# A fixed order on VectorE in the closing norm of each stage, held weight splits, and three smaller moves in a two-block transformer kernel

## The chip, the cores and the metric

The kernel runs on 1 core of one Trainium2 chip. The metric is the device time of one execution in microseconds (us); of several runs the median is taken. A core has five engines that work side by side, each on its own queue of instructions: TensorE (PE in the profile, its weight loads PEld), VectorE (DVE), ScalarE (ACT), GpSimd (POOL) and SyncE (SP). SP only issues transfers here.

## The reference, cut to what matters

The input is one sequence of 256 tokens with 1024 features, in fp32. Ten stages follow one another, and each ends in the same way:

```python
for l in range(2):
    x = layer_norm(ALPHA * x + 0.5 * swiglu(x, ffn1_w1[l], ffn1_w2[l]))   # 1024 -> 2 x 2816 -> 1024
    x = layer_norm(ALPHA * x + token_mix(x))      # three attention branches, each with its gate
    x = layer_norm(ALPHA * x + 0.5 * swiglu(x, ffn2_w1[l], ffn2_w2[l]))
for l in range(2):
    x = layer_norm(ALPHA * x + (ssd_mixer, dilated_attention)[l](x))
    x = layer_norm(ALPHA * x + moe(x))            # 32 experts, 2 per token, hidden 512
```

The third attention branch of token_mix subtracts from its scores a running sum over the tokens of `log_sigmoid(f + b_f)`; this sum is called its decay below.

## The kernel before, in words

**Products.** Every fp32 product is made of three products of parts. A raw weight tile of 1 MB comes by a transfer from SP into one of 4 buffers (`NRAW`). `split` (L63) makes of a piece of 128 x 2 x 512 a high part with a copy on ScalarE (L65) and a low part with a subtraction on VectorE (L66), in one of 7 split buffers (`NSPLIT`). `mm3` (L115) multiplies high by high (L116), high by low (L117) and low by high (L118). The activations lie transposed, as high part `xh` and low part `xl`.

**Feed-forward pass** (`ffn`, L275, four times). 11 groups of 256 columns. Group G does: gate_up(G) (L294), four splits and 48 products into one tile of two PSUM banks (`gu`); gating (L306), a tanh on ScalarE (L190) and two products on VectorE (L309, L310); then, from G = 2, the down products of group G - 2, 24 of them into four banks (`acc`, one for each half of 128 tokens and half of 512 columns); then `turned` (L313), which transposes the gated group (`hT`, L317) and splits it (L320, L321). So in groups 0 and 1 no down products lie between a gate/up sum and its transposes, and the one `gu` tile has to be read before the next sum begins. Behind the last group the down products of the last two groups are left as the tail.

**The end of a stage** (`finish`, L213). `tail_half` (L90) issues the last products, for token half t = 0, then 1; inside each k both column halves take turns, so that both end together. The tail is 4 k deep in feed-forward, 2 in token_mix (`MTAIL`, L846), 3 in SSD (`TAIL`, L1049), 2 in the dilated attention (`DTAIL`). For each token half VectorE then does, by column half, the residual sum (L241) and its statistics (L242), then the aggregation (L244); ScalarE a logarithm and an exponential (L247, L248); VectorE the centring of the whole row (L251), three small steps (L252 to L254) and, by column half, the scaling (L263; L260 where the columns are dealt out in another order). TensorE transposes each scaled half row (`turn_x`, `xps`, L181); ScalarE copies the high part (L183) and VectorE subtracts the low part (L184). The last norm of the program writes its rows out instead.

**Order.** The instructions of each engine are put in a fixed order when the program is built, by a list scheduler with its own cost estimates, which takes what it holds to be ready first. An edge of the kind `order` (L57) only fixes the order of two instructions in that list. The splits of the next stage, which need its weights alone, can be placed before, between or behind the instructions of a norm.

**Set-up in the first feed-forward pass.** At groups 2, 5 and 8 (`SETUPG`) parts of `setup_all` run: POOL loads constants, tables, parameters (`load_params`, `pars`) and the routers' weights `rw` (L1237, L1238). `router_parts` (L1243) splits `rw` into `rs` on ScalarE (L1246) and VectorE (L1247). It is called before the SSD and the dilated stage (L1603); the scheduler has placed the first call's two instructions into the first feed-forward pass.

**token_mix** (L435). The projections come in 256-column groups. The decay block (L670 to L677) stands before the compressed scores of the first branch: log_sigmoid in 17 small VectorE instructions and an exponential, two products with a triangle of ones (L673, L674), a negation (L675) and a store from ScalarE's queue. Its readers come in the third branch.

**MoE** (L1250). Behind the router's arithmetic, in which the tokens' places are gathered, 16 pairs of experts run at a steady pace. A pair does gate products `gps` and up products `ups` (L1430), tanh, two VectorE products (`t`, L1438, L1439), transposes (L1441), a copy on VectorE (`hT`, L1444), down products `yp` (L1453) and their copy (L1459), and adds to `eacc` (L1464) at the end of the stage. Its weights lie in 21 slots in a written order (`ORDER`, L23): 8 tiles in space freed by other things (a0 to a7), the 4 raw tiles (r), the 7 split buffers (s) and the two activation tiles (x0, x1). The last pair of the first MoE stage is followed by the splits of the dilated stage.

Of the kernel before, what the change touches and what calls it, by code (L numbers as in the profile page):

```python
# [10 lines left out]
F32 = mybir.dt.float32  # L11
# [30 lines left out]
def tile_stack(ctx: ExitStack, tc: tile.TileContext, a: dict, out: bass.AP):  # L42
# [89 lines left out]
    pars = const.tile([128, 256], F32)  # L132

    def load_params(pp, pq):
# [20 lines left out]
        for i in range(2):  # L155
            ps = pq.tile([128, 128], F32, tag="tr", name="ptr")
            nc.tensor.transpose(ps, stage[i], ident)
            nc.vector.tensor_copy(out=pars[:, i * 128:(i + 1) * 128], in_=ps)
# [18 lines left out]
    def turn_x(trp, t, hf, src, tag):  # L177
# [5 lines left out]
        nc.scalar.activation(out=X["h"][:, t, cs, :], in_=ps, func=AF.Copy)  # L183
        nc.vector.tensor_tensor(out=X["l"][:, t, cs, :], in0=ps, in1=X["h"][:, t, cs, :].bitcast(F32), op=ALU.subtract)  # L184
# [28 lines left out]
    def finish(accs, last, scale, g, b, trp, tag="tr", room=None, dealt=False, was_dealt=False, write=None, loaded=False):  # L213


        with pool(name="lnt", bufs=2) as tmp, ExitStack() as own:
# [15 lines left out]
            for t in range(2):  # L232
                st = tmp.tile([128, 2, 6], F32, tag="st", name="lnst")
                for hf in range(2):
                    hs = slice(hf * 512, (hf + 1) * 512)
                    k = X["k"][:, t, hs]
                    if was_dealt:
                        nc.vector.scalar_tensor_tensor(out=r[:, t, hs].rearrange("p (f k) -> p f k", k=4), in0=by_rows(k), scalar=ALPHA * scale,  # L238
                                                       in1=accs[t][hf].rearrange("p (f k) -> p f k", k=4), op0=ALU.mult, op1=ALU.add)
                    else:  # L240
                        nc.vector.scalar_tensor_tensor(out=r[:, t, hs], in0=k, scalar=ALPHA * scale, in1=accs[t][hf], op0=ALU.mult, op1=ALU.add)  # L241
                    nc.vector.bn_stats(out=st[:, hf, :], in_=r[:, t, hs])  # L242
                mv = tmp.tile([128, 2], F32, tag="mv", name="lnmv")
                nc.vector.bn_aggr(out=mv, in_=st)  # L244
                rs = tmp.tile([128, 1], F32, tag="rs", name="lnrs")
                nw = tmp.tile([128, 1], F32, tag="nw", name="lnnw")
                nc.scalar.activation(out=rs, in_=mv[:, 1:2], func=AF.Ln, bias=eps_t[scale], scale=1.0)  # L247
                nc.scalar.activation(out=rs, in_=rs, func=AF.Exp, scale=-0.5)  # L248
                if t == 1:
                    table("exp_and_others")  # L250
                nc.vector.scalar_tensor_tensor(out=r[:, t, :], in0=r[:, t, :], scalar=mv[:, 0:1], in1=gb[:, 0, :], op0=ALU.subtract, op1=ALU.mult)  # L251
                nc.vector.scalar_tensor_tensor(out=nw, in0=mv[:, 1:2], scalar=eps_t[scale], in1=rs, op0=ALU.add, op1=ALU.mult)  # L252
# [1414 lines left out]
```

## Time and profile before

| | before |
|---|---|
| time, median of 3 runs (lowest to highest) | 2876.24 us (2873.5 to 2877.69) |
| the profiled execution's own time | 2875.49 us |
| its span in the trace | 2873.7 us |
| mean granted TensorE clock | 0.97 |
| instructions in the span | 36446 |
| bytes moved by transfers | 710.37 MB, 247 GB/s over the span |

The span is the time from the first to the last instruction in the trace. A busy share is an engine's busy time over the span. The granted clock is TensorE's clock as a share of full speed (2.4 GHz); 0.50 is its lower level, 1.2 GHz. "A <- B" behind an idle time names what ended it.

### The profile page before, as it was taken

To read this page: it belongs to the slowest core of one execution; us is meant where nothing else is said; L and a number is where in the kernel's file an instruction comes from. 1 tells how busy PE (TensorE), PEld (TensorE's weight loads), DVE (VectorE), ACT (ScalarE), POOL (GpSimd) and SP (SyncE) were. 2 spreads that over 40 slices of the span, in tenths; PEclk is the share of its full clock that TensorE was granted. 3 is DMA by queue.
4 is the path that set the end of the run, shared out by engine and by line. 5 is a ranking of instruction groups with operands and counts; after the bars stand their busy time and mean duration, and the time that the engine had idled before them with its cause. 6 is when DMAs were issued, how large, how long until landed. Compare 5 with 4: busy or idle time off the path is not lost. (4 is left out here: it accounts for less than half of the span.)

```text
span 2873.7 us, 36446 instructions
## 1 busy us (share of the span) xinstructions
PE 2721.6 (95%) x14368; PEld 1890.8 (66%) x14368; DVE 1345.2 (47%) x2669; ACT 991.6 (35%) x1699; POOL 57.9 (2%) x124
## 2 busy tenths in 40 slices
PE   8799999899999999989989989999998989999997
PEld 6687688788788768878878854444436975444443
DVE  4466665655655566665578841111116662111112
ACT  3343555444444355544447710100014440000011
POOL 2100000000000000000000000000000000000000
PEclk9899999999999999999999989999998998999999
DMA  8765454565555645446555599999974468999993
GB/s 217 209 212 155 116 174 162 168 191 188 163 191 175 168 124 171 155 150 198 172 164 177 190 375 421 421 421 421 421 296 152 129 231 359 420 420 421 421 421 148
DMA packets 302944, 710.37 MB, mean 247 GB/s; under 512 B 21189, under 2 KB 212353, under 8 KB 253617
## 3 DMA queue, kind: packets, MB, share of 16 engines
q1 hardware_dynamic: 289920, 688.11, 65.7%
q10 hardware_dynamic: 10736, 14.80, 1.6%
q0 software_dynamic: 2112, 5.08, 1.2%
q8 instruction: 115, 1.88, 0.3%
q14 instruction: 61, 0.49, 0.1%
HBM read 706.81 MB, written 4.27 MB: 247 GB/s over the span
## 5 line engine op out<-in xcount | busy, mean ns | idle before, releaser
L66 DVE TENSOR_TENSOR whl<-w,whl 128x1024 fp32r<-128x1024 f32 x487 | 590.7, 1217 | 401.6 <-ACT whl L65 400.1
L65 ACT ACTIVATE whl<-w 128x1024 fp32r<-128x1024 f32 x487 | 510.1, 1053 | 511.2 <-PE gu L118 177.3
L116 PE MATMUL pp<-xh,whl 128*128 128x256 f32 (+1 forms) x1048 | 301.4, 288 | 4.8 <-DVE cv L909 3.2
L117 PE MATMUL pp<-xl,whl 128*128 128x256 f32 (+1 forms) x1048 | 302.9, 289 | 0.0
L118 PE MATMUL pp<-xh,whl 128*128 128x256 f32 (+1 forms) x1048 | 298.7, 285 | 0.0
L116 PE MATMUL gu<-whl,xh 128*128 128x512 f32 x704 | 284.3, 404 | 4.3 <-ACT xh L183 2.4
L117 PE MATMUL gu<-whl,xh 128*128 128x512 f32 x704 | 279.6, 397 | 0.8 <-DVE whl L66 0.8
L118 PE MATMUL gu<-whl,xl 128*128 128x512 f32 x704 | 279.7, 397 | 0.3 <-DVE xl L184 0.3
L116 PEld LDWEIGHTS pp<-xh,whl 128*128 128x128 f32 (+1 forms) x1048 | 199.0, 190 | 11.4 <-issue 5.1
L117 PEld LDWEIGHTS pp<-xl,whl 128*128 128x128 f32 (+1 forms) x1048 | 199.0, 190 | 3.4 <-issue 1.7
L118 PEld LDWEIGHTS pp<-xh,whl 128*128 128x128 f32 (+1 forms) x1048 | 198.8, 190 | 1.8 <-issue 0.9
L1438 DVE SCALAR_TENSOR_TENSOR t<-t,gps 128x512 f32<-128x512 f32 x32 | 22.0, 688 | 345.2 <-ACT t L190 345.2
L116 PEld LDWEIGHTS gu<-whl,xh 128*128 128x128 f32 x704 | 135.5, 192 | 32.8 <-ACT xh L183 3.8
L118 PEld LDWEIGHTS gu<-whl,xl 128*128 128x128 f32 x704 | 135.2, 192 | 31.2 <-DVE xl L184 1.6
L117 PEld LDWEIGHTS gu<-whl,xh 128*128 128x128 f32 x704 | 135.3, 192 | 28.3 <-DVE whl L66 1.1
L1407 PEld LDWEIGHTS xgp<-ot,xk 128*128 128x128 f32 x1024 | 121.4, 194 | 36.9 <-issue 24.3
L1407 PE MATMUL xgp<-ot,xk 128*128 128x128 f32 x1024 | 132.6, 284 | 6.5 <-ACT xg L1391 6.5
L116 PE MATMUL acc<-whl,hhi 128*128 128x512 f32 x352 | 137.3, 390 | 0.0
L118 PE MATMUL acc<-whl,hlo 128*128 128x512 f32 x352 | 137.1, 389 | 0.0
L117 PE MATMUL acc<-whl,hhi 128*128 128x512 f32 x352 | 137.0, 389 | 0.0
L1517 DVE TENSOR_TENSOR ogt<-ot,gt 128x128 f32<-128x128 f32 x64 | 15.8, 287 | 257.9 <-PE ogp L1420 237.7
L1459 ACT ACTIVATE y<-yp 128x512 f32<-128x512 f32 x64 | 38.2, 597 | 276.2 <-PE yp L1453 276.2
(496 smaller groups left out, 4582.5 us busy)
## 6 DMA issues: line engine op xcount, KB each, us to landing
w<-in_ffn_w_dram SPq DMA_DIRECT2D x176, 512.0 KB, 4.8
wa<-in_moe_w_up_dram SPq DMA_DIRECT2D x55, 1024.0 KB, 12.8
wa<-in_moe_w_gate_dram SPq DMA_DIRECT2D x48, 1024.0 KB, 12.8
whl<-in_moe_w_down_dram SPq DMA_DIRECT2D x45, 1024.0 KB, 12.7
w<-in_ffn_w_dram SPq DMA_DIRECT2D x44, 1024.0 KB, 4.9
wa<-in_moe_w_down_dram SPq DMA_DIRECT2D x44, 1024.0 KB, 11.8
whl<-in_moe_w_gate_dram SPq DMA_DIRECT2D x42, 1024.0 KB, 12.6
whl<-in_moe_w_up_dram SPq DMA_DIRECT2D x39, 1024.0 KB, 14.0
```

Source lines behind the costliest of these rows:

```text
L65: nc.scalar.activation(out=hi, in_=w, func=AF.Copy)
L66: nc.vector.tensor_tensor(out=lo, in0=w, in1=hi.bitcast(F32), op=ALU.subtract)
L116: nc.tensor.matmul(out=o, lhsT=wh, rhs=xh, start=first, stop=False, skip_group_check=skip)
L117: nc.tensor.matmul(out=o, lhsT=wh, rhs=xl, start=False, stop=False, skip_group_check=skip)
L118: return nc.tensor.matmul(out=o, lhsT=wl, rhs=xh, start=False, stop=last, skip_group_check=skip)
L1407: ms.append(nc.tensor.matmul(out=ps[:, c, 0:P], lhsT=xt[:, i, (q * 4 + c) * 128:(q * 4 + c + 1) * 128], rhs=os[i], start=(i == 0), stop=(i ...
L1438: nc.vector.scalar_tensor_tensor(out=t[0:P], in0=t[0:P], scalar=1.0, in1=gps[0:P], op0=ALU.add, op1=ALU.mult)
L1459: nc.scalar.activation(out=ys[hf][0:P], in_=yp[0:P], func=AF.Copy)
L1517: nc.vector.tensor_tensor(out=og, in0=o, in1=gt[:, i, 2 * q:2 * q + 2].unsqueeze(2).to_broadcast([128, 2, CAP]), op=ALU.mult)
```

## The change

The norm of `finish` is written as one chain on VectorE, each instruction ordered behind the one before (`dve`, `follow`), with the centring in two column halves. `tail_half` ends one column half before it begins the other. `after_norm` counts the splits behind a norm: the first four may be placed anywhere, save behind a MoE stage, where they stand behind its last tanh (ScalarE) and its last `hT` copy (VectorE); the fifth to eighth stand behind the norm's last exponential (ScalarE) and the chain's last instruction (VectorE). `split_pair`, the split of two 64-column pieces in token_mix, counts too. There are 8 split buffers, and the tails of SSD and token_mix are 4 deep; one tile of the freed space in MoE makes room, the slots stay 21, and the parameter tile shrinks. In feed-forward the gate/up sum of group 1 goes into the banks of `acc0`, and the output tiles are made behind gating(1). The router split is ordered behind the last norm before it. The decay block stands behind the second branch.

```diff
@@ constants @@
-ORDER = ("a7 r r r r a6 a5 a4 s s s s s s s a3 a2 a1 a0 x0 x1", "a7 a6 r r r r a5 a4 a3 a2 a1 s s s s s s s a0 x0 x1")
+ORDER = ("a6 r r r r a5 a4 a3 s s s s s s s s a2 a1 a0 x0 x1", "a6 a5 r r r r a4 a3 a2 a1 a0 s s s s s s s s x0 x1")
-NSPLIT = 7
-TAIL = 3
-MTAIL = 2
+NSPLIT = 8
+AT_HAND = 4
+TAIL = 4
+MTAIL = 4
@@ split @@
+    def follow(x, *before):
+        for y in before:
+            if y is not None:
+                tc.add_manual_dep(x.ins, y.ins.name, order, reason="order")
+        return x
+    def after_norm(act, dve):
+        n = behind.get("n", 99)
+        behind["n"] = n + 1
+        if n < AT_HAND:
+            follow(act, behind.get("act0"))
+            follow(dve, behind.get("dve0"))
+        elif n < NSPLIT:
+            follow(act, behind["act"])
+            follow(dve, behind["dve"])
     def split(w, shape):
         hi, lo = split_tile(shape)
-        nc.scalar.activation(out=hi, in_=w, func=AF.Copy)
-        nc.vector.tensor_tensor(out=lo, in0=w, in1=hi.bitcast(F32), op=ALU.subtract)
+        after_norm(nc.scalar.activation(out=hi, in_=w, func=AF.Copy),
+                   nc.vector.tensor_tensor(out=lo, in0=w, in1=hi.bitcast(F32), op=ALU.subtract))
@@ tail_half @@
-            for n, k in enumerate(ks):
-                acc_half(accs, t, *k, first=False, last=(n == len(ks) - 1))
+            ts = slice(t * 128, (t + 1) * 128)
+            for hf in range(2):
+                hs = slice(hf * 512, (hf + 1) * 512)
+                for n, (wh, wl, mh, ml) in enumerate(ks):
+                    mm3(accs[t][hf], mh[:, ts], ml[:, ts], wh[:, hs], wl[:, hs], first=False, last=(n == len(ks) - 1), skip=True)
@@ load_params @@
-    pars = const.tile([128, 256], F32)
+    pars = const.tile([128, 136], F32)
@@ finish @@
+        behind["act0"], behind["dve0"] = before
...
+            def dve(x):
+                chain[0] = follow(x, chain[0])
+                return x
...
+            def summed(t, hf):
...
+                    dve(V.scalar_tensor_tensor(out=z, in0=k, scalar=ALPHA * scale, in1=accs[t][hf], op0=ALU.mult, op1=ALU.add))
+                dve(V.bn_stats(out=sm[t][0][:, hf * 6:hf * 6 + 6], in_=z))
+            def centred(t):
+                st, mv, rs, nw = sm[t]
+                dve(V.bn_aggr(out=mv, in_=st.rearrange("p (h s) -> p h s", h=2)))
+                nc.scalar.activation(out=rs, in_=mv[:, 1:2], func=AF.Ln, bias=eps_t[scale], scale=1.0)
+                x = nc.scalar.activation(out=rs, in_=rs, func=AF.Exp, scale=-0.5)
+                if t == 1:
+                    behind["act"] = x
...
-                nc.vector.scalar_tensor_tensor(out=r[:, t, :], in0=r[:, t, :], scalar=mv[:, 0:1], in1=gb[:, 0, :], op0=ALU.subtract, op1=ALU.mult)
+                    dve(V.scalar_tensor_tensor(out=r[:, t, hs], in0=r[:, t, hs], scalar=mv[:, 0:1], in1=gb[:, 0, hs], op0=ALU.subtract, op1=ALU.mult))
...
+            summed(0, 0)
+            summed(0, 1)
+            centred(0)
+            lows = [scaled(0, hf) for hf in range(2)]
+            summed(1, 0)
+            if write is None:
+                dve(lows[0])
+                dve(lows[1])
+            summed(1, 1)
+            centred(1)
+            lows = [scaled(1, hf) for hf in range(2)]
+            if write is None:
+                dve(lows[0])
+                dve(lows[1])
+            behind["dve"] = chain[0]
+            behind["n"] = 0
@@ ffn @@
-            accs = acc_tiles(aps, "acc")
...
-                gu = gps.tile([128, 2, 512], F32, tag="gu", name="gu")
+                if G == 1:
+                    gu = aps.tile([128, 2, 512], F32, tag="acc0", name="gu1")
+                else:
+                    gu = gps.tile([128, 2, 512], F32, tag="gu", name="gu")
...
                 e = gating(gate_up(G))
+                if G == 1:
+                    two = [aps.tile([128, 2, 512], F32, tag=f"acc{t}", name=f"acc{t}") for t in range(2)]
+                    accs = [[a_[:, hf, :] for hf in range(2)] for a_ in two]
@@ token_mix: the decay block, unchanged in itself, moves from before the compressed scores to here @@
             branch_out(1, a["w_br_b"][l], True, oh, ol, gt)
+            lf = log_sigmoid(wk, fx, [128, 2, 8])
...
+            nc.scalar.dma_start(out=ncd, in_=ncum)
             q_c = q_chunks(load(w_in, 2072), load(w_in, 2328), "qc", pair=False)
@@ router_parts @@
-        nc.scalar.activation(out=rs[:, :, 0:36], in_=rw[:, l], func=AF.Copy)
-        nc.vector.tensor_tensor(out=rs[:, :, 36:72], in0=rw[:, l], in1=rs[:, :, 0:36].bitcast(F32), op=ALU.subtract)
+        follow(nc.scalar.activation(out=rs[:, :, 0:36], in_=rw[:, l], func=AF.Copy), behind["act"])
+        follow(nc.vector.tensor_tensor(out=rs[:, :, 36:72], in0=rw[:, l], in1=rs[:, :, 0:36].bitcast(F32), op=ALU.subtract), behind["dve"])
@@ moe @@
-    AHEAD = 8
+    AHEAD = 7
...
                 tanh(out=t[0:P], in_=gps[0:P], scale=0.5)
+                done["t"] = last_tanh[-1]
...
-                nc.vector.tensor_copy(out=hT[:, :, 0:P], in_=ht[:, :, 0:P])
+                done["hT"] = nc.vector.tensor_copy(out=hT[:, :, 0:P], in_=ht[:, :, 0:P])
...
-            finish(accs, combine, 1.0, g_, b_, mp, tag="m", room="left", was_dealt=True, write=out if write else None)
+            finish(accs, combine, 1.0, g_, b_, mp, tag="m", room="left", was_dealt=True, write=out if write else None, before=(done["t"], done["hT"]))
```

## Rows read from the trace of the kernel before

**Rows 1.** The page's first part: busy time of each engine.

```profile
PE 2721.6 (95%) x14368; PEld 1890.8 (66%) x14368; DVE 1345.2 (47%) x2669; ACT 991.6 (35%) x1699; POOL 57.9 (2%) x124
```

**Rows 2.** Waits of TensorE: line, releaser, us in total, times, longest.

```profile
PE xps L181 <- DVE xk L263: 33.8, 10, 7.6
PE hT L317 <- DVE sg L310: 26.8, 6, 14.4
```

**Rows 3.** Waits between 60 and 95 us.

```profile
ACT rs L1246 <- DMA rw<-moe_w_router_expert_dram: 21.6, 1, 21.6
```

**Rows 4.** Stretches: A:B length, busy us (count) by engine, granted clock, DMA share, GB/s.

```profile
65.00:75.00 10.00, 10.00 (x46) 8.28 (x45) 0.28 (x1) 0.00 (x0) 0.75 (x1) 1.00 0.84 0
75.00:86.50 11.50, 2.51 (x12) 1.73 (x10) 0.42 (x1) 0.89 (x2) 3.35 (x6) 0.70 0.41 113
77.51:91.90 14.39, 0.00 (x1) 0.01 (x1) 5.29 (x7) 5.66 (x7) 5.17 (x8) 0.57 0.47 108
91.90:105.69 13.79, 13.79 (x53) 11.36 (x54) 7.62 (x7) 4.62 (x5) 0.00 (x0) 0.83 0.80 268
```

**Rows 5.** Stretches behind a first gating, first and third feed-forward pass.

```profile
29.68:35.20 5.52, 5.52 (x15) 4.55 (x16) 3.05 (x3) 3.03 (x4) 0.00 (x0) 0.50 0.69 205
758.83:762.24 3.41, 3.41 (x10) 2.63 (x9) 1.83 (x2) 1.28 (x2) 0.00 (x0) 0.50 0.69 282
```

**Rows 6.** Stretches at ends of stages, engines in order PE, PEld, DVE, ACT, POOL.

```profile
221.36:226.81 5.45, 5.45 (x25) 4.17 (x23) 5.38 (x10) 3.46 (x5) 0.00 (x0) 1.00 0.00 2
226.81:238.61 11.80, 9.71 (x41) 6.97 (x40) 11.59 (x21) 4.63 (x7) 0.00 (x0) 0.86 0.59 158
537.41:560.16 22.75, 16.20 (x64) 12.83 (x64) 15.34 (x27) 8.69 (x13) 2.54 (x9) 0.77 0.30 95
736.86:754.66 17.80, 14.54 (x64) 10.37 (x64) 13.74 (x23) 7.67 (x11) 0.00 (x0) 1.00 0.56 182
1445.52:1456.98 11.46, 3.04 (x18) 2.41 (x17) 10.12 (x18) 4.63 (x7) 0.00 (x0) 0.77 0.87 271
2170.90:2183.44 12.54, 3.74 (x17) 3.13 (x16) 11.18 (x23) 4.07 (x8) 1.62 (x6) 0.68 0.21 59
2357.38:2385.05 27.67, 16.70 (x68) 14.75 (x68) 18.83 (x74) 4.48 (x10) 0.00 (x0) 0.54 0.80 328
2857.86:2870.46 12.60, 2.48 (x6) 0.76 (x4) 12.45 (x22) 3.11 (x6) 0.00 (x0) 0.78 0.11 42
```

**Rows 7.** A norm, 730.5 to 750.2: groups, tiles lnst and lnnw; transposes from 1446.72.

```profile
L66 DVE TENSOR_TENSOR whl<-w,whl 128x1024 fp32r<-128x1024 f32 x4 | 4.8, 1204 | 0.0
L263 DVE SCALAR_TENSOR_TENSOR xk<-xk,lnrs,gb 128x512 f32<-128x512 f32 x4 | 2.8, 746 | 0.0
L241 DVE SCALAR_TENSOR_TENSOR xk<-xk,acc 128x512 f32<-128x512 f32 x4 | 2.7, 682 | 2.3 <-PE acc L118 2.3
...
730.50:750.20 19.70, 3.06 (x6) 1.00 0.37 121
...
730.50:750.20 19.70, 1.05 (x6) 1.00 0.37 121
...
L183 ACT ACTIVATE xh<-xps 128x512 fp32r<-128x512 f32 x4 | 2.4, 598 | 5.6 <-PE xps L181 5.4
...
1446.72 1.29 PE L181 MATMUL xps<-ident,xk 128*128 128x128 f32 x8 [1.20 <-DVE xk L263]
```

**Rows 8.** Stretches: last pair of the first and of the second MoE stage.

```profile
2150.81:2167.27 16.46, 9.67 (x37) 3.65 (x37) 5.96 (x7) 3.77 (x4) 0.00 (x0) 0.79 0.66 207
2847.17:2856.71 9.54, 7.80 (x37) 3.26 (x37) 1.38 (x2) 0.60 (x1) 0.00 (x0) 1.00 0.31 110
```

**Rows 9.** The decay block: its stretch, and the group of the negation.

```profile
306.00:329.00 23.00, 16.83 (x70) 9.63 (x69) 17.56 (x92) 10.86 (x37) 0.32 (x1) 0.70 0.34 108
...
L675 DVE TENSOR_SCALAR ncum<-pt 8x256 f32<-8x256 f32 x1 | 0.4, 412 | 1.1 <-PE pt L674 1.1
```

**Rows 10.** SP's issues, 2100 to 2120: start, us, line, out<-in.

```profile
2110.64 3.34 SPq L1499 DMA_DIRECT2D w<-in_moe_w_down_dram  x2
```

More of the change, by code (lines that the diff above doesn't have):

```diff
@@ L157, in load_params @@
             nc.tensor.transpose(ps, stage[i], ident)
-            nc.vector.tensor_copy(out=pars[:, i * 128:(i + 1) * 128], in_=ps)
+            n = (128, 8)[i]
+            nc.vector.tensor_copy(out=pars[:, i * 128:i * 128 + n], in_=ps[:, 0:n])
     def col(name, i):
@@ L211, in by_rows, with finish @@
         return ap.rearrange("p (k f) -> p f k", k=4)
-    def finish(accs, last, scale, g, b, trp, tag="tr", room=None, dealt=False, was_dealt=False, write=None, loaded=False):
+    def finish(accs, last, scale, g, b, trp, tag="tr", room=None, dealt=False, was_dealt=False, write=None, loaded=False, before=(None, None)):
+        behind["act0"], behind["dve0"] = before
         with pool(name="lnt", bufs=2) as tmp, ExitStack() as own:
@@ L231, in finish, with flat @@
                 new_x()
-            for t in range(2):
-                st = tmp.tile([128, 2, 6], F32, tag="st", name="lnst")
+            V = nc.vector
+            sm = [[tmp.tile([128, n], F32, tag=k, name=k) for k, n in (("st", 12), ("mv", 2), ("rs", 1), ("nw", 1))] for t in range(2)]
+            chain = [None]
+            def dve(x):
+                chain[0] = follow(x, chain[0])
+                return x
+            def flat(x):
+                return x.rearrange("p (f k) -> p f k", k=4)
@@ L234, in finish @@
+            def centred(t):
[5 more added lines that the diff above has]
+                    behind["act"] = x
+                    table("exp_and_others")
                 for hf in range(2):
                     hs = slice(hf * 512, (hf + 1) * 512)
-                    k = X["k"][:, t, hs]
@@ L237, in finish @@
[L237 to L250, printed above, removed]
@@ new lines, in centred, with scaled @@
+                dve(V.scalar_tensor_tensor(out=nw, in0=mv[:, 1:2], scalar=eps_t[scale], in1=rs, op0=ALU.add, op1=ALU.mult))
+                dve(V.scalar_tensor_tensor(out=nw, in0=nw, scalar=-0.5, in1=rs, op0=ALU.mult, op1=ALU.mult))
+                dve(V.scalar_tensor_tensor(out=rs, in0=nw, scalar=1.5, in1=rs, op0=ALU.add, op1=ALU.mult))
+            def scaled(t, hf):
+                hs = slice(hf * 512, (hf + 1) * 512)
+                y, bias, rs = r[:, t, hs], gb[:, 1, hs], sm[t][2]
+                k = y if write is not None else X["k"][:, t, hs]
+                if dealt:
+                    dve(V.scalar_tensor_tensor(out=by_rows(k), in0=flat(y), scalar=rs, in1=flat(bias), op0=ALU.mult, op1=ALU.add))
+                else:
+                    dve(V.scalar_tensor_tensor(out=k, in0=y, scalar=rs, in1=bias, op0=ALU.mult, op1=ALU.add))
+                if write is not None:
+                    (nc.sync, nc.scalar)[hf].dma_start(out=write[t * 128:(t + 1) * 128, hs], in_=y)
+                    return None
+                return turn_x(trp, t, hf, k, tag)[1]
@@ L794, in token_mix @@
             branch_out(1, a["w_br_b"][l], True, oh, ol, gt)
+            lf = log_sigmoid(wk, fx, [128, 2, 8])
+            ncum = ap_.tile([8, S], F32, name="ncum")
+            ps = ptp.tile([8, S], F32, tag="pt", name="pt")
+            nc.tensor.matmul(out=ps, lhsT=lf[:, 0, :], rhs=tri, start=True, stop=False, skip_group_check=True)
+            nc.tensor.matmul(out=ps[:, 128:256], lhsT=lf[:, 1, :], rhs=tri[:, 0:128], start=False, stop=True, skip_group_check=True)
+            nc.vector.tensor_scalar(out=ncum, in0=ps, scalar1=-1.0, scalar2=None, op0=ALU.mult)
+            ncd = tabp.tile([8, S], F32, name=f"ncd{l}")
+            nc.scalar.dma_start(out=ncd, in_=ncum)
             q_c = q_chunks(load(w_in, 2072), load(w_in, 2328), "qc", pair=False)
```

38 lines of the change are left out of this document (10 added, 28 removed).

## The prediction, made before the changed kernel ran

> **What bounds the kernel.** I read the page's head first: TensorE is busy for 2721.6 us [rows 1] of the span of 2873.7, so the time is TensorE's work, the 152 us in which it stands, and what it loses at the lower of its two clocks. Then its waits [rows 2]: 33.8 us for the scaled half rows that the norm leaves on VectorE, and 26.8 us, six times, for the gating of a gate/up sum, one of these alone 14.4. Both are waits for VectorE, which is busy less than half of the span: its order is what counts, not its load. Then one stretch per edit, as a table of stretches with the granted clock.
>
> **Router split (L1246, L1247).** In the first feed-forward pass ScalarE waits 21.6 us for the router's weights [rows 3], and VectorE, whose part of the split needs ScalarE's, stands behind it; the tanh of the gating and three weight splits are queued behind them, and TensorE stands from 77.51 to 91.90 [rows 4]. The change ties both instructions behind the last norm of the feed-forward part, when the weights are long there; on both queues the SSD stage's later splits then stand behind them, 0.45 us. What is late next is a transfer: between 65 and 75 us the DMA engines move nothing, and the next megabyte of feed-forward weights comes between 75 and 86.5 [rows 4]. Half of the next group (24 products, 5.45 us) can run at 77.51 + 0.65 for transposes; the other half waits until about 86.3 + 1.06 + 0.2 = 87.5, then runs some 7 us, partly at the low clock: it ends near 94.5 instead of 105.69 [rows 4]. Term **-11**. Ends: -2 (everything slips with the DMA) and -17 (no transfer in the way: 14.4 and the low clock's share of the 13.79 us after it, a third at half speed, 2.4).
> By the page "Trainium Kernel Development and Optimization", Key Constraints, of the Trainium skill, transfers issued from SP, ACT and POOL run on the same 16 DMA engines and interleave, so that these weights would have come beside POOL's set-up loads; the stretch at 0 GB/s speaks against it. By that rule the term would be -17 and the sum 6 us lower.
>
> **Second gate/up sum in the output banks.** It frees TensorE from waiting for the first gating in each of four passes: 26.8 - 14.4 = 12.4 us in the five other waits [rows 2], of which I take 12. Behind them the clock was at half for 5.52 us of work in the first pass and 3.41 in the third [rows 5], as much in the fourth: 2.8 + 1.7 + 1.7 = 6.2. The second sum needs four more splits; the eighth split buffer holds them, and they are ready before the first sum ends only if VectorE is through with the norm (below). The output tiles are made when the second gating has read its banks; the third gate/up sum runs meanwhile. 18.2 in all, term **-17**; ends -18 and -8 (the splits late in half the passes).
>
> **Entry to a stage.** T is the end of a tail. 24 of its products take 5.45 us [rows 6]. Now both column halves of a token half end together and the two token halves interleave on VectorE with up to four splits of 1.20 us [rows 7]. With the tail ordered by column half, the second of four quarters ends at T - 5.45. VectorE in its fixed order, by [rows 7]: a sum takes 0.68, the statistics and aggregation of a token half 3.06 / 2 = 1.53 (0.67 a quarter and 0.2), its small steps 1.05 / 2 = 0.53, a scaling 0.75, and a half centring, the same operation and size, some 0.7. Sum and statistics of the second quarter end at T - 4.1; aggregation, centring and small steps take 2.1, so T - 1.95; two scalings T - 0.5; the third quarter T + 0.9. Eight transposes take 1.29 us at full clock [rows 7], ScalarE's copy 0.6: the first token half is there from T + 1.35, its low parts, each as long as a sum, at T + 2.0 and T + 2.65. Behind these low parts VectorE's queue now holds the fourth quarter: T + 4.0, centred T + 6.15, scaled T + 6.9 and T + 7.6. TensorE has done the first half's 24 products at T + 7.0, transposes, and begins the second half at T + 8.3, ending the group at T + 13.9. Against that:
> - feed-forward to mixing, twice: 11.80 to the second half [rows 6], now 8.3: -7.
> - mixing to feed-forward, twice, where the tail was two products deep and is now four: 22.75 [rows 6] and 22.3 to the group's end, now 13.9; I take 8 each: -16.
> - feed-forward to feed-forward: 17.80 [rows 6], now 13.9: -3.5.
> - feed-forward to SSD, whose first products need both token halves: 11.46 [rows 6], now 7.9: -3.5.
> Together **-30**, ends -35 and -15 (half the gain eaten by waits between the engines). The four held splits start when VectorE is done, T + 9.5, the first is ready at T + 10.7, and TensorE asks for it at T + 13.9: no cost while this slack of 3 us holds. Into the two routers the same order counts less, since the last token half ends the path: 27.67 us from the tail to the gather before the second [rows 6]; chain end T + 11.1 against T + 13, and 0.45 for the router split that stood in the first: **-4.5**, ends -8 and 0. The deeper SSD tail gives back nothing: its parts are ready before.
>
> **MoE to the dilated stage.** In the last pair of the first MoE stage 16.46 us lie between the gate/up products and the last product, in the second 9.54 [rows 8]; the difference is splits of the next stage ahead of the pair's tanh and products. The change puts four behind them, the others behind the norm: **-6.5**, ends -7 and 0. Then the norm: both quarters of a token half come nearly together, all 16.7 us of VectorE work lie on the path, and the low parts now come before the fourth quarter: 12.54 us [rows 6] grow to about 14. **+1.5**, ends -1 and +4. The last norm, 12.60 us [rows 6], cannot overlap its halves any more: **+1**, ends -0.5 and +2.5.
>
> **Decay block of the third branch.** Moved from the compressed scores to behind the second branch: 17 small VectorE instructions, one Exp, two small products, and on ScalarE's queue one store of 0.3 us, past the bias loads. Its readers come 12 projections later. In the stretch of 23.0 us TensorE is busy for 16.83 and stands for 6.2 [rows 9]; each small step costs 0.085 in the queue (1.4 us), the negation 0.4 and the 1.1 it waits [rows 9], the products 1.3. Much of it fills holes: **-3** for both layers, ends -8 and +2.
>
> **At nothing.** The MoE slots stay 21 (one more split buffer, one tile fewer ahead): the stage's last weights are asked for at 2110.64 [rows 10], some 48 us ahead of their products, so that TensorE's pace of 29.5 us a pair is kept and a start a few microseconds earlier is passed on whole. The narrower parameter tile lies under feed-forward products.
>
> **Sum.** -11 - 17 - 30 - 4.5 - 6.5 + 1.5 + 1 - 3 = -69.5. The profiled execution took 2875.5, 0.7 below the median shown: 2806.0, on the median's scale **2807**.
>
> **Rivals.**
> *The weights flow* (2801): as above, if the DMA pause moves or shrinks. Chance 0.08.
> *The norm only changes its waits* (2837): the entries and the routers gain nothing, because VectorE now stands in its fixed order for TensorE's transposes, which stand behind the tail: 2807 + 30. For it: in 11.80 us of the entry VectorE is busy for 11.59 [rows 6]. Against: 4.8 of them are splits that leave. Chance 0.13.
> *The order is not what it says* (2858): the edges bind only the order within one engine; if the scheduler had other reasons for the early router split and the late norm, only the second sum remains: 2876 - 17. Chance 0.03.
> *Slower* (2887): at the seven entries to projecting stages the fifth to eighth split start only behind the norm's last instruction. If VectorE gets there late, TensorE stands for the lateness, and the next group (10.9 us) runs at half clock, 5.5 lost. It outweighs 69.5 from 9.9 us an entry, a lateness of 4.4 us, the fifth split at T + 18.3 instead of T + 10.7; at 6 us it is 7 x 11.5 = 80. For it: the norm that now takes longest, into the dilated stage, ends 14 us after T. Against: there the four at hand last until T + 24. Chance 0.04; a lateness around 4.4 us gives no change, 0.02.
>
> **Numbers.** Forecast 0.70, its own range 2787 to 2829 (the terms' bounds sum to 2782 and 2860, and not all fall on one side). Reaching to the norm rival, the range is 2787 to 2842. A measurement of this kernel can tell about 0.2% from no change: faster 0.94, same 0.02, slower 0.04.
>
> **What would show it.** Right: no router split between 60 and 95 us, and in its place one wait of about 4 us for a weight split near the end of the DMA pause; waits for the gating below 5 us in all; the transposes wait less than 20 us for the scaled rows; mixing to feed-forward near 14 us; the last pair's transposes wait below 1 us. Wrong: a second wait behind L66 or L65 at the entries, half clock there for longer than now, or the pause of the DMA engines gone.

## The result, and the profile after

The changed kernel takes **2839.62 us** (median of 4 runs, 2838.07 to 2843.96) against 2876.97 for the kernel before in the same comparison: the ratio is 0.987, 95% interval 0.9849 to 0.9891, so it is 1.3% faster, by 37 us. The forecast was 2807 with the range 2787 to 2842. The time lies just inside, but only because the range was drawn out for a rival: the forecast's own range, 2787 to 2829, was missed, and about half of the forecast gain came. The profiled execution is the longest of the four (2843.96, span 2842.2), some 4 us above the median.

The page's first part and TensorE's waits in the profile of the changed kernel answer to [rows 1] and [rows 2]:

```profile
PE 2715.3 (96%) x14368; PEld 1886.6 (66%) x14368; DVE 1354.7 (48%) x2689; ACT 986.3 (35%) x1699; POOL 57.8 (2%) x124
```

```profile
PE xps L204 <- DVE xk L298: 25.3, 9, 6.2
PE xps L204 <- DVE xk L296: 12.3, 3, 6.2
PE hT L371 <- DVE sg L364: 9.6, 3, 4.2
...
PE pt L1204 <- ACT rf L1201: 5.8, 2, 5.3
PE gu L138 <- DVE xk L273: 4.5, 2, 2.3
```

The waits for the gating fell from 26.8 to 9.6 us. Those for scaled rows hardly moved: plain rows from 33.8 to 25.3, but the dealt rows (L260 before, L296 now) stand at 12.3, where they were 8.6. One wait has grown, for `rf` in the dilated stage (0.5 us before), and one is new, for a sum of the norm (L273) ahead of a gate/up product.

The stretches of the changed kernel that answer to [rows 4, 6, 8], in the columns of those groups:

```profile
62.00:74.00 12.00, 10.40 (x46) 8.26 (x45) 3.78 (x4) 3.33 (x4) 2.24 (x3) 1.00 0.76 7
90.40:121.27 30.87, 25.35 (x86) 17.98 (x85) 17.61 (x29) 12.23 (x15) 2.79 (x6) 0.78 0.59 193
...
528.77:545.57 16.80, 14.54 (x66) 11.91 (x64) 12.77 (x20) 7.96 (x11) 2.53 (x9) 0.90 0.31 97
719.77:737.17 17.40, 15.51 (x66) 11.76 (x66) 14.09 (x25) 7.96 (x11) 0.00 (x0) 0.90 0.17 62
...
2112.01:2121.48 9.47, 7.83 (x36) 3.20 (x36) 3.64 (x4) 0.70 (x1) 0.00 (x0) 1.00 0.68 223
2126.68:2141.16 14.48, 3.88 (x17) 3.23 (x17) 12.71 (x25) 6.29 (x11) 0.98 (x4) 0.59 0.40 98
2321.59:2351.30 29.71, 16.67 (x66) 14.74 (x67) 19.99 (x76) 4.79 (x11) 0.00 (x0) 0.54 0.78 312
2824.88:2838.94 14.06, 2.48 (x6) 0.76 (x4) 13.57 (x24) 3.11 (x6) 0.00 (x0) 0.77 0.10 37
```

In order: the DMA engines are held for 12 us at 7 GB/s, much as before; in the first pass 30.87 us lie between the ends of the gate/up sums of groups 4 and 5; mixing to feed-forward 16.80 (22.75 before); feed-forward to feed-forward 17.40 (17.80); the last pair of the first MoE stage 9.47 (16.46); the norm into the dilated stage 14.48 (12.54); the tail before the second router up to the gather 29.71 (27.67); the last norm 14.06 (12.60).

To see where time went, the span is cut at the end of every tail (the last output product ahead of a norm's transposes, from TensorE's timeline). Lengths in us, of the profiled executions; the first begins with TensorE's first instruction, at about 7 us. b3 and c2 are experiments below:

| stage, up to the end of its tail | before | changed | b3 | c2 |
|---|---|---|---|---|
| feed-forward 1 | 219.9 | 215.1 | 212.8 | 200.3 |
| mixing 1 | 310.6 | 306.6 | 304.5 | 303.5 |
| feed-forward 2 | 199.4 | 191.0 | 188.3 | 188.2 |
| feed-forward 3 | 197.1 | 191.6 | 190.1 | 188.5 |
| mixing 2 | 310.9 | 306.6 | 306.1 | 303.2 |
| feed-forward 4 | 200.6 | 191.0 | 188.1 | 188.1 |
| SSD | 218.3 | 218.3 | 217.8 | 214.9 |
| MoE 1 | 507.1 | 499.4 | 499.6 | 498.6 |
| dilated attention | 186.5 | 194.9 | 191.2 | 193.3 |
| MoE 2 | 503.0 | 505.8 | 503.4 | 503.4 |
| last norm and output | 13.4 | 14.8 | 13.6 | 13.6 |

A stretch at the lower clock comes in some executions and not in others, and is worth up to 1.7 us (half of the 3.41 us of [rows 5]). The entry from mixing to feed-forward, 16.80 us here at a granted clock of 0.90, takes 15.20 at 1.00 in run a4 below, whose edit does not touch it. So single differences below 2 us mean little, and the changed kernel's lengths, from its longest execution, are some 4 us too long in all.

### The profile page after: what moved, and what is told of

Read it like the earlier page. It is cut to its first block, busy times and chain, and to the rows that moved or that the text cites. A ratio compares the mean times of both kernels' runs of the same rounds, so it can differ in the third digit from the quotient of the medians.

```text
span 2842.2 us, 36460 instructions
## 1 busy us (share of the span) xinstructions
PE 2715.3 (96%) x14368; PEld 1886.6 (66%) x14368; DVE 1354.7 (48%) x2689; ACT 986.3 (35%) x1699; POOL 57.8 (2%) x124
## 5 line engine op out<-in xcount | busy, mean ns | idle before, releaser
L84 ACT ACTIVATE whl<-w 128x1024 fp32r<-128x1024 f32 x487 | 505.9, 1051 | 455.1 <-PE gu L140 129.0
```

The source lines that it names most:

```text
L84: after_norm(nc.scalar.activation(out=hi, in_=w, func=AF.Copy), nc.vector.tensor_tensor(out=lo, in0=w, in1=hi.bitcast(F32), op=ALU.subtract))
```

## The experiments

All times are medians of 4 runs (d1: of 10), and ratios are to the kernel before; the changed kernel stands at 0.987. The intervals reach some 5 us to each side: a1 and a3 are not told apart from the changed kernel, and b2's slowest run (2838.04) only just lies below its fastest (2838.07).

| kernel | us | ratio, 95% interval |
|---|---|---|
| a1 router split free | 2837.70 | 0.9852 (0.9836 to 0.9869) |
| a2 one gate/up sum | 2851.90 | 0.9900 (0.9882 to 0.9919) |
| a3 eight at hand behind MoE | 2839.45 | 0.9859 (0.9843 to 0.9875) |
| a4 neighbouring skip weights | 2826.67 | 0.9825 (0.9803 to 0.9846) |
| b1 four one-bank tiles | 2833.00 | 0.9840 (0.9820 to 0.9860) |
| b2 gate/up banks first | 2835.36 | 0.9848 (0.9829 to 0.9867) |
| b3 no fixed order | 2824.90 | 0.9809 (0.9789 to 0.9829) |
| b4 eight at hand everywhere | 2857.32 | 0.9920 (0.9903 to 0.9937) |
| c1 decay block back | 2848.71 | 0.9896 (0.9879 to 0.9912) |
| d1 before, tie alone | 2876.81 | 0.9993 (0.9982 to 1.0004) |
| d2 before, neighbouring skip weights | 2861.43 | 0.9943 (0.9923 to 0.9963) |
| c2 the parts that help, together | 2803.66 | 0.9733 (0.9717 to 0.9750) |

### The first pass: the tie on the router split (d1, a1)

d1 is the kernel before with two edges, behind the norm's last exponential (`behind["act"]`) and its last scaling (`behind["dve"]`); a1 is the changed kernel without its two.

```diff
+        tc.add_manual_dep(x.ins, behind["act"].ins.name, order, reason="order")
+        tc.add_manual_dep(y.ins, behind["dve"].ins.name, order, reason="order")
```

```diff
-        follow(nc.scalar.activation(out=rs[:, :, 0:36], in_=rw[:, l], func=AF.Copy), behind["act"])
+        nc.scalar.activation(out=rs[:, :, 0:36], in_=rw[:, l], func=AF.Copy)
...
```

> The kernel before with the router split's tie alone. Theory A (the DMA standstill of 62 to 77 us sets the end): TensorE's wait of 14.4 us goes, but weights are late for the next two groups, the tail of the first pass ends at 221 to 225 us instead of 226.8: 2 to 6 us faster, 2870-2875. Rival B (the tie frees the whole wait): the tail ends at 210 to 216 us, 2860-2866.

> The changed kernel without its edges on the router split. Theory A (the weights are the limit): the DMA engines move nothing between about 64 and 74 us in both kernels, so the first feed-forward pass ends when the late weights let it, whichever queue waits for them; the tie is worth little: the tail of the first pass ends at 222 to 226 us (222.2 with the tie), the time rises by 0 to 4 us to 2840-2844. Rival B (the tie is worth its 11 to 14 us and another part of the change took them back): the tail ends at 232 or later, the time is 2850 or more.

**The tie alone is worth nothing that can be measured** (0.9993). The pass up to its tail is 218.6 us long against 219.9. ScalarE's timeline in d1 shows what stands in the place of the wait of [rows 3] (start, length, instruction, idle time before it):

```profile
86.11 2.00 ACT L65 ACTIVATE whl<-w 128x1024 fp32r<-128x1024 f32 x2 [22.53 <-DMA w<-in_ffn_w_dram]
88.02 0.58 ACT L190 ACTIVATE sg<-gu 128x512 f32<-128x512 f32 x1
```

Where ScalarE waited 21.6 us for the router's weights it now waits 22.53 for the next group's, in a split that stands ahead of the same tanh. So TensorE's wait for the gating is 14.9 us here, as it was 14.4:

```profile
PE hT L318 <- DVE sg L311: 14.9, 1, 14.9
```

The tail ends at 225.4 us, and both theories of d1 placed it too early: theory A was right that the late transfer sets the end, and too generous even so.

a1 ends its first pass at 223.5 us, as theory A said, but it does not repeat the early split, so it says nothing of the tie: without it the scheduler puts ScalarE's two instructions at 1228 and 1639 us. With the second router split out of the entry of the dilated stage, that stage is 191.0 us long instead of 194.9, its wait for `rf` 2.9 instead of 5.3. The router split is not shown to be the cause: b3 has the same 2.9 us and 191.2 with the split in the entry, and c2 waits 5.6 us and takes 193.3 with the split out of it.

### What holds the DMA engines (a4, d2)

```diff
-        d = a["ssd_d_2"][0].rearrange("(j t) -> t j", t=2)
-        for t in range(2):
-            nc.gpsimd.dma_start(out=dcol[t * 64:t * 64 + 64], in_=d[t].unsqueeze(0).to_broadcast([64, 16]))
+        nc.gpsimd.dma_start(out=drow, in_=a["ssd_d_2"].to_broadcast([128, HS]))
```

VectorE then takes every second value of `drow` where it halved `dcol`.

> The changed kernel, but the SSD skip weights come as 32 neighbouring values a partition instead of two transfers of 2048 single 4-byte pieces, and VectorE picks the 16 it needs. Theory A (these pieces hold the DMA engines): the standstill of about 12 us is gone, TensorE's waits of 4.2 and 4.1 us for the gating and the slow fifth group go, and the tail of the first pass ends 8 to 17 us earlier than 222.2: 2823-2832. Rival B (other set-up loads hold them, the routers' 16-byte pieces above all): the standstill stays longer than 6 us and the tail moves by less than 4 us.

> The kernel before with the SSD skip weights as neighbouring values alone (no tie, no other part of the change). Theory A (the 4-byte pieces are the root): POOL no longer waits 7.6 and 9.1 us for them, the routers' weights come in time, TensorE's wait of 14.4 us goes without any tie, and the first pass up to its tail (219.9 us) is 14 to 20 us shorter: 2858-2865. Rival B (the router split stands badly in any case): the wait for the gating stays above 8 us and the pass is shorter by under 7 us.

Theory A in both. The stretch from 62 to 74 us in a4, beside the first row of the stretches above:

```profile
62.00:74.00 12.00, 12.00 (x57) 9.94 (x56) 6.65 (x7) 4.51 (x5) 5.13 (x8) 1.00 0.85 177
```

The engines are about as busy (0.85 against 0.76), but move 177 GB/s instead of 7. What held them shows in the list of transfers issued between 50 and 90 us, first of the changed kernel, then of a4 (KB each, us from issue to landing):

```profile
dcol<-in_ssd_d_dram POOLq DMA_DIRECT2D x2, 4.0 KB, 18.2
```

```profile
drow<-in_ssd_d_dram POOLq DMA_DIRECT2D x1, 16.0 KB, 6.3
```

Two transfers of 4 KB read every second value; of their packets the trace holds 32 in the kernel before, with 256 bytes (64 values) each and a median of 8.4 us. Spread evenly, 32 x 8.4 / 16 engines would be an estimated 17 us of every engine. Four times the bytes, read as neighbours, take 6.3 us. The Trainium skill, page "DMA: Bandwidth & Descriptors", section "Rules for kernel authors", says that a strided last dimension lowers to one descriptor for each element and should be rearranged to be contiguous. The two runs agree with the advice: the first pass is 13.6 us shorter in a4 and 18.0 in d2. Descriptors do not show in the trace, which has packets of 64 values. In d2 the wait for the router's weights is 5.7 us instead of 21.6, with the split where it was, and TensorE's wait of 14.4 us for the gating is gone without any tie.

### The second gate/up sum and its two-bank tiles (a2, b1)

a2 undoes the part, b1 keeps the second sum and gives each half of it and each output sum a tile of one bank:

```diff
+            accs = acc_tiles(aps, "acc")
...
-                if G == 1:
-                    gu = aps.tile([128, 2, 512], F32, tag="acc0", name="gu1")
...
```

```diff
-                    gu = aps.tile([128, 2, 512], F32, tag="acc0", name="gu1")
+                    gu = [aps.tile([128, 512], F32, tag=f"acc{t}", name=f"gu1{t}") for t in range(2)]
...
-                    two = [aps.tile([128, 2, 512], F32, tag=f"acc{t}", name=f"acc{t}") for t in range(2)]
-                    accs = [[a_[:, hf, :] for hf in range(2)] for a_ in two]
+                    accs = acc_tiles(aps, "acc")
```

> The changed kernel with the second gate/up sum in the usual tile again and four output tiles of one bank. Theory A (joined banks): the sum in the output banks saved 2.5, 5.4 and 4.1 us in passes two to four, and made the two column halves of a token half one tile, so that the norm's first sum waits for both; with four tiles the first sum starts at T - 8.2 instead of T - 4.5 (T: end of the tail) and TensorE's first wait behind the tail falls from 1.4 us to under 0.5. Together 6 to 12 us slower: 2845-2852. Rival B (the wait comes from the order of the products alone, not from the tile): the first sum still starts later than T - 6, the 1.4 us stay, 12 to 18 us slower: 2852-2858.

> The changed kernel with the second gate/up sum kept in the output banks, but in two tiles of one bank (its gating in two halves), and four output tiles of one bank. Theory A (joined banks): the norm's first sum starts at about T - 7.2 as with one sum, TensorE's first wait behind the four feed-forward tails falls from 1.4 us to under 0.5, and nothing of the 12 us of the second sum is lost: 5 to 10 us faster than the changed kernel, 2830-2835. Rival B (the one-sum kernel's shorter stages came from its later clock or splits): under 2 us, 2838-2841.

Theory A in both, though a2's first sum starts at T - 7.2 and not T - 8.2. From a2 to b1 only the second sum differs: 2851.9 - 2833.0 = 18.9 us is its worth. From b1 to the changed kernel only the tiles differ: joining the two column halves costs 6.6. VectorE's timeline at the end of the second pass, of the changed kernel (tail's end T = 719.77) and of b1 (T = 716.21):

```profile
715.28 0.69 DVE L273 SCALAR_TENSOR_TENSOR xk<-xk,acc 128x512 f32<-128x512 f32 x1 [4.01 <-PE acc L140]
716.00 0.69 DVE L274 BATCH_NORM_STATS2 st<-xk 128x6 f32<-128x512 f32 x1
716.61 0.67 DVE L273 SCALAR_TENSOR_TENSOR xk<-xk,acc 128x512 f32<-128x512 f32 x1
```

```profile
708.99 0.69 DVE L273 SCALAR_TENSOR_TENSOR xk<-xk,acc 128x512 f32<-128x512 f32 x1 [1.29 <-PE acc L140]
709.71 0.69 DVE L274 BATCH_NORM_STATS2 st<-xk 128x6 f32<-128x512 f32 x1
710.81 0.69 DVE L273 SCALAR_TENSOR_TENSOR xk<-xk,acc 128x512 f32<-128x512 f32 x1 [0.40 <-PE acc L140]
```

In b1 the second column half waits by itself (0.40) and its sum starts at T - 5.4. In the changed kernel the first sum starts at T - 4.5, the second follows with no wait of its own at T - 3.2: the norm's first sum waits for the whole two-bank tile. The remaining 0.9 us is four products of token half 1, which the scheduler has put into TensorE's order between those of half 0: only 20 of its 24 follow the product that ends the wait. That order was not tried by itself.

What the tiles cost shows in the entry from feed-forward to feed-forward, up to the end of the next group's sum, at full clock. First a4, whose tiles are joined as in the changed kernel, then b1:

```profile
703.32:719.48 16.16, 14.16 (x65) 10.85 (x66) 14.09 (x25) 7.85 (x11) 0.00 (x0) 1.00 0.19 66
```

```profile
716.21:730.14 13.93, 13.56 (x66) 10.63 (x64) 11.86 (x20) 7.74 (x11) 0.00 (x0) 1.00 0.21 76
```

With single tiles the group ends at T + 13.93, in the fixed order.

### The fixed order (b3) and the bank that it hands on late (b2)

b3 and b2, each on the changed kernel:

```diff
-                chain[0] = follow(x, chain[0])
+                chain[0] = x
```

```diff
-        with pool(name="accps", bufs=1, space=PSUM) as aps, pool(name="gups", bufs=1, space=PSUM) as gps, \
+        with pool(name="gups", bufs=1, space=PSUM) as gps, pool(name="accps", bufs=1, space=PSUM) as aps, \
```

> The changed kernel without the edges of the norm's fixed order on VectorE (the instructions and the held splits stay). Theory A (the order carries the gain of the entries): the scheduler puts low parts and splits between the norm's instructions again; the entries from mixing to feed-forward are 3 us or more longer each, 5 to 15 us slower, 2845-2855. Rival B (the deeper tail and the held splits carry it, the order costs at the last norm and at the dilated stage): within 3 us or faster, 2832-2842.

> The changed kernel with the gate/up tile's two banks opened ahead of the output banks. Theory A (a bank handed on late): at the entry from mixing to feed-forward the first gate/up product waits 2.3 us because its banks are those of the mixing's last two output tiles, the second of which the fixed order reads only behind the first half's low parts; with other banks the wait falls under 0.8 and each entry (15.2 to 16.8 us from the tail to the group's end, by the clock) is 1.6 to 3.3 us shorter: 2833-2837. Rival B (the wait is for the first half's parts themselves): no change within 1 us at these entries, 2838-2841.

**Without the fixed order the kernel is 14.7 us faster**: rival B, beyond what it expected. In the table of stages the gains over 2 us that have a norm in them are in mixing 1 (2.1 us), in feed-forward 2 and 4 (2.7 and 2.9), the dilated stage (3.7) and the second MoE stage (2.4), and the last norm, 14.8 us long in all nine kernels with the order, takes 13.6. The first pass, which has no norm ahead of it, is 2.3 shorter too: that is not the order. VectorE's timeline at the end of the second pass, of the changed kernel (T = 719.77) and of b3 (T = 712.78):

```profile
721.58 0.68 DVE L273 SCALAR_TENSOR_TENSOR xk<-xk,acc 128x512 f32<-128x512 f32 x1
722.30 0.69 DVE L274 BATCH_NORM_STATS2 st<-xk 128x6 f32<-128x512 f32 x1
722.91 1.27 DVE L207 TENSOR_TENSOR xl<-xps,xh 128x512 fp32r<-128x512 f32 x2
724.10 0.68 DVE L273 SCALAR_TENSOR_TENSOR xk<-xk,acc 128x512 f32<-128x512 f32 x1
```

```profile
712.82 0.16 DVE L289 SCALAR_TENSOR_TENSOR rs<-nw,rs 128x1 f32<-128x1 f32 x1
712.90 0.68 DVE L273 SCALAR_TENSOR_TENSOR xk<-xk,acc 128x512 f32<-128x512 f32 x1
713.49 1.41 DVE L298 SCALAR_TENSOR_TENSOR xk<-xk,rs,gb 128x512 f32<-128x512 f32 x2
714.82 0.69 DVE L274 BATCH_NORM_STATS2 st<-xk 128x6 f32<-128x512 f32 x1
715.42 0.67 DVE L273 SCALAR_TENSOR_TENSOR xk<-xk,acc 128x512 f32<-128x512 f32 x1
716.01 1.28 DVE L207 TENSOR_TENSOR xl<-xps,xh 128x512 fp32r<-128x512 f32 x2
```

The scheduler puts one sum of the second token half (L273 at 712.90) before the scalings of the first and the other (715.42) before its low parts (L207), while these wait for TensorE and ScalarE; the written order keeps the last sum behind the low parts. That has a second price at the entry from mixing to feed-forward. TensorE's timeline there, of the changed kernel and of b2:

```profile
531.91 0.75 PE L138 MATMUL gu<-whl,xh 128*128 128x512 f32 x1 [2.26 <-DVE xk L273]
```

```profile
527.34 0.50 PE L138 MATMUL gu<-whl,xh 128*128 128x512 f32 x1 [0.25 <-ACT xh L206]
```

The gate/up tile lies in the banks of the mixing's last two output tiles, and the sum that reads the last one comes late in the fixed order. With other banks the wait is 0.25 us, and the entry takes 14.15 and 14.17 us up to the end of the group's sum instead of 16.80 and 16.78: theory A, 4.3 us by the medians. Not all of that is the bank. Here are a4, with the bank as in the changed kernel, and b2, both at full clock:

```profile
513.89:529.09 15.20, 12.94 (x66) 10.63 (x64) 12.70 (x20) 7.74 (x11) 2.53 (x9) 1.00 0.34 104
```

```profile
526.22:540.37 14.15, 13.78 (x65) 10.65 (x64) 11.92 (x20) 7.74 (x11) 2.53 (x9) 1.00 0.23 76
```

So the bank is worth about 1 us an entry, and the other 1.6 are the clock of the changed kernel's profiled execution (0.90). In b3 the same two entries take 13.95 and 13.91 us without touching the banks.

### Splits behind the norm (b4, a3)

b4 everywhere, a3 behind the MoE stages alone:

```diff
-AT_HAND = 4
+AT_HAND = 8
```

```diff
-        if n < AT_HAND:
+        if n < (AT_HAND if behind.get("act0") is None else NSPLIT):
```

> The changed kernel with all eight splits allowed ahead of the norm's end everywhere (the fixed order of the norm's own instructions stays). Theory A (holding splits back protects the norm, as at the dilated stage, where eight at hand put 4.7 us into it): entries after feed-forward and mixing 1 to 3 us longer, 5 to 15 us slower, 2845-2855. Rival B (buffers and weights hold the later splits anyway): stages but the dilated one change by less than 0.5 us, 2837-2841.

> The changed kernel, but behind a MoE stage all eight splits may stand ahead of the norm (behind the last tanh and hT copy), not four. Theory A (the held splits displace the rope tables): the dilated stage, 8.4 us longer than before, loses because splits 5 to 8 stand on VectorE between the small steps of the rope tables; with eight at hand TensorE's wait of 5.3 us for ScalarE's copy is gone and the stage is 5 to 8 us shorter, 2832-2835. Rival B (the norm in its fixed order is what is longer): the stage is within 1.5 us of the changed kernel's 194.9, 2838-2841.

b4 is 17.7 us slower, a little above theory A: with the fixed order in place, holding four splits back is what protects the norm. Without that order it was not tried. VectorE's timeline in b4 shows how they come in, one split between each two small steps:

```profile
725.81 0.21 DVE L287 SCALAR_TENSOR_TENSOR nw<-mv,eps,rs 128x1 f32<-128x1 f32 x1
725.95 1.22 DVE L85 TENSOR_TENSOR whl<-w,whl 128x1024 fp32r<-128x1024 f32 x1
727.08 0.15 DVE L288 SCALAR_TENSOR_TENSOR nw<-nw,rs 128x1 f32<-128x1 f32 x1
727.15 1.21 DVE L85 TENSOR_TENSOR whl<-w,whl 128x1024 fp32r<-128x1024 f32 x1
```

At the dilated stage the account is even. In the changed kernel splits 5 onwards stand between the small steps of the rotary tables, which the stage needs at once:

```profile
2145.13 0.29 DVE L1139 CAST ang<-posi 128x256 f32<-128x256 int32 x1
2145.34 1.22 DVE L85 TENSOR_TENSOR whl<-w,whl 128x1024 fp32r<-128x1024 f32 x1
2146.47 0.35 DVE L1140 TENSOR_SCALAR ang<-ang,fr 128x256 f32<-128x256 f32 x1
2146.87 1.22 DVE L85 TENSOR_TENSOR whl<-w,whl 128x1024 fp32r<-128x1024 f32 x1
```

TensorE then waits 5.3 us for `rf`, a copy of ScalarE that comes at 2160.0, just behind the first instructions that use the tables (L1174 at 2158.6). With eight at hand (a3) this wait is gone, but the splits stand in the norm, and TensorE waits for the first scaled rows 9.07 us instead of 4.35 (the changed kernel, then a3):

```profile
2131.03 1.94 PE L204 MATMUL xps<-ident,xk 128*128 128x128 f32 x8 [4.35 <-DVE xk L298]
```

```profile
2134.23 1.94 PE L204 MATMUL xps<-ident,xk 128*128 128x128 f32 x8 [9.07 <-DVE xk L298]
```

The stage is 1.1 us shorter, which is rival B's number, but not for its reason: the held splits do displace the tables, and putting them ahead only changes where VectorE is late.

### The decay block (c1), and the parts that help (c2)

c1 moves the block back; c2 holds the edits of a1, a4, b1, b2 and b3 together.

```diff
             nc.vector.tensor_copy(out=fx, in_=pt[:, :, 24:32])
+            lf = log_sigmoid(wk, fx, [128, 2, 8])
...
+            nc.scalar.dma_start(out=ncd, in_=ncum)
...
             branch_out(1, a["w_br_b"][l], True, oh, ol, gt)
-            lf = log_sigmoid(wk, fx, [128, 2, 8])
...
-            nc.scalar.dma_start(out=ncd, in_=ncum)
```

> The changed kernel with the decay block back before the compressed scores. Theory A (the move, not the entry, shortened the mixing stages by 4.0 and 4.3 us): both mixing stages are 2.5 to 4.5 us longer than 306.6, the time is 2845-2849. Rival B (the block was filling holes, the entry gained): under 1 us each, 2839-2842.

> The changed kernel without the norm's fixed order and without the router's tie, with four one-bank output tiles, the gate/up banks opened first, and the SSD skip weights as neighbouring values. If the savings seen one by one add up (14.7 without the order, 13 for the weights, 4 for the tiles of which the order may have been the cause of half, 2 to 4 for the second router split at the dilated stage): 2803-2811. If they overlap (the tiles and banks only matter under the fixed order): 2811-2815. Over 2815: two of them disturb each other.

c1: theory A. Both mixing stages are about as long as before (310.6 and 310.3), and the kernel is 9 us slower; 4.0 and 3.7 us are in these stages. TensorE's waits in the first of them, of the changed kernel and of c1, show where the block stood in the way:

```profile
PE sc L761 <- DVE m L766: 2.0, 3, 0.9
```

```profile
PE sc L769 <- DVE m L774: 4.2, 2, 3.2
PE pt L762 <- DVE cs L759: 2.1, 1, 2.1
```

So what the entry from feed-forward to mixing gained did not reach the end of the stage. With single tiles (b1) both mixing stages are 2.3 and 2.2 us shorter than in the changed kernel.

c2 takes 2803.66 us, at the low end of the first expectation: the savings add up for the most part. Seen one by one the five edits gave 40.5 us (14.7, 13.0, 6.6, 4.3 and 1.9), together 36.0; the expectation had counted the tiles and banks at 4. c2 beats both kernels, the one before by 2.7%. In it TensorE's waits for scaled rows are

```profile
PE xps L204 <- DVE xk L298: 12.4, 7, 6.5
PE xps L204 <- DVE xk L296: 11.4, 5, 4.6
```

23.8 us together, against 37.6 in the changed kernel; waits for the gating are no longer among the first.

## Why the prediction was right or wrong

The sum said -69.5; the two spans differ by 31.5, the medians by 37. The time reached the stretched range, but not for the reasons given: of the signs that the prediction named for being right, two held, that no router split stands between 60 and 95 us and that the last pair's transposes wait below 1 us (0.9). The others did not: ScalarE's wait for a weight split is 14.9 us instead of about 4, the gating 9.6 instead of below 5, the scaled rows 37.6 instead of below 20, and mixing to feed-forward 16.8 instead of near 14. Term by term:

**Router split, -11: wrong.** d1 gives -1.3 in the pass. The step that failed is that half of the next group "can run at 77.51 + 0.65 for transposes": it took TensorE to be free once the router split was gone. But the tanh stands on ScalarE behind weight splits, and these wait for the same late megabyte. The next megabyte was read rightly as what is late next; that it holds the gating through ScalarE's queue was not. Nor do the engines rest in the stretch at 0 GB/s: its share is 0.84 [rows 4], and a4 and d2 show what holds them. The rival "the weights flow" rested on the right cause, and its condition came true only in a4 and d2, where the strided transfer was taken away.

**Second sum, -17: right.** From the end of the first gate/up sum to the end of the second the four passes are 6.3, 2.5, 5.4 and 4.1 us shorter, 18.3 together; by a2 and b1 it is 18.9. Its side effect, the joined tiles, the text had not: "The output tiles are made when the second gating has read its banks" was costed at nothing and took 6.6, which fell on the entries.

**Entry to a stage, -30: mostly wrong**, about -12 came, nearly all of it from mixing to feed-forward (22.75 to 16.80; two of them, -6.0 and -5.5, of -16). Behind a feed-forward tail the step that failed is "Sum and statistics of the second quarter end at T - 4.1": with joined tiles the first sum started only at T - 4.5, two waits in one, they ended at T - 1.8, and all behind them came 2.4 us late. The first rows were turned at T + 1.4 instead of T, and TensorE waited there 1.38 us. From mixing to feed-forward the tiles are single and the first rows were in time; there the prediction had no wait for a bank, and that of the gate/up tile was late. The rest of the working stands: with the tiles taken apart (b1) or the banks changed (b2) the next group ends at T + 13.93 and at T + 14.15 and 14.17, where the prediction had T + 13.9. From feed-forward to mixing the term was also read from the wrong row: of the 11.80 us [rows 6] 9.71 were work, so that no more than 2.1 of standing could go, and when the projections ahead of the compressed scores end, 0.4 and 1.0 us are left of the gain.

**Routers, -4.5: wrong for the second.** The fixed order made the last token half later: 27.67 to 29.71 us, and 28.3 in b3 without it. The first gained 1.9 (24.6 to 22.7 from the tail to the gather; 22.6 in b3).

**Last MoE pair, -6.5: right** (20.1 to 14.7 us to the tail's end, -5.4). **Dilated entry, +1.5: mis-sized.** The norm itself grew by 1.9, as said; the stage lost 8.4, since splits that had stood ahead of the norm now meet the rotary tables on VectorE. The prediction looked at the fifth split's lateness for TensorE, and not at what else stands behind it on VectorE. How the 8.4 us divide between the norm, the held splits and the router split stays open: the stage is 191.0 to 196.4 us long in the variants of the changed kernel, and taking parts away (a1, a3, b3, c2) never brings back the 186.5. **Last norm, +1:** +1.5. **Decay block, -3: too small**; 7.7 by c1, so less of it had filled holes. The steps were also priced too low: in the trace of the kernel before log_sigmoid has 15 on VectorE, not 17, of 0.12 to 0.24 us each, not 0.085.

Of the rivals, "the norm only changes its waits" came nearest (2837), but its condition did not hold: the entries from mixing gained, and in the fixed order VectorE waits at most 0.3 us before the low parts of a first token half. b3 shows that the fixed order costs time, by what it places ahead of the last sum, not that VectorE stands in it for TensorE. That the time fell near 2837 comes from terms that missed and gained elsewhere, and is luck. The slower rival did not occur: TensorE's waits for a split of L84 stayed below 2 us.

## What to carry to other kernels

An order written out by hand on one engine fixes when every buffer that it reads comes free: here it cost 14.7 us against the scheduler's own order, while keeping four foreign instructions (weight splits) out of the chain gained 17.7 with that order in place; the two should be tried apart. When a wait is removed, read what the waiting engine's queue holds next: the tanh behind the router split was also behind weight splits that waited for the same transfer. Two tiles joined into one also join their waits. A stage's length from one execution is compared only with the granted clock beside it: 1.6 us of an entry were the clock.

## What the runs showed of the hardware that was not expected

Two transfers of 4 KB that read every second 4-byte value hold the 16 DMA engines for some 12 us (7 GB/s between 62 and 74 us, at a busy share of 0.76), and a transfer of neighbouring values four times as large does not (177 GB/s). That one set-up load was worth 13 us in the changed kernel and 16.6 in the kernel before, more than most parts of the change.
